# Transposes of an attention step ahead of its score blocks, another ring for one row tile, and two operand addresses moved

## The chip, the cores and the metric

The kernel runs on one core of one Trainium2 chip, in one launch. The metric is the device time of one execution in microseconds (us). The kernel before takes 2876.37 us, the median of three runs (2876.22 to 2876.55).

## What is computed

One layer of a transformer for two streams, 256 context tokens and 2048 latent tokens, with parameters shared. Cut to what matters here:

```python
h = rms_norm(x, norm1_g) * (1 + sc1) + sh1
q, k, v, f = project(h, w_in, q_g, k_g)        # 4 heads x 2 halves x 64 | same | 4 x 128 | 4 x 128
# attention of a head: two score halves, one difference of softmaxes
s = einsum('bqhmd,bkhmd->bhmqk', q, k) * scale  # m = 0, 1; latent: 2048 queries, 2560 keys
p = softmax(s)
a = p[:, :, 0] - lam * p[:, :, 1]
o = einsum('bhqk,bkhe->bqhe', a, v)
# the other half of the width
spec = fft2(f, axes=(positions, 128 channels), norm='ortho').real
mix = concat([rms_norm(o) * (1 - lam_init), spec @ w_four]) @ w_out
x = x + g1 * mix
x = x + g2 * relu(h2 @ w1) ** 2 @ w2            # h2: the second norm of x
```

## The kernel before

All matrix work is fp32 or split in two fp32r parts (`h` for high, `l` for low), of which three products are added. The program runs in stages: modulation and projections of 18 token tiles of 128 rows (up to about 465 us), the Fourier half (465 to 526), attention of four heads (526 to some 1260), output projection, and an MLP in three parts (to 2873).

**Projection and Fourier.** `v_out` (L397) copies the value rows of a token tile out of PSUM (L402, ScalarE) into a row tile `vo` and stores it (L403, the SyncE queue, written SP or SPq). The row tile comes from the ring `t2`, six tiles of 2 KB a partition in the pool of the projection; another ring of the same pool, `ff`, has four tiles and holds the rows that the Fourier channels load and store (`fh`, `fo`, `mid`). The pool ends with the projection, and the tiles of the Fourier stage are laid over its addresses. The first subtraction of the Fourier stage, four instructions `d<-ss,ss` on VectorE (DVE) at L845 (`diff`), takes differences of loaded rows `ss`; TensorE (PE) then reverses rows (`rev<-d`, L859), transforms (`pabo`, L786; `py`, `pz`, L751 and L753), and ScalarE (ACT) and DVE combine (`yd`, L770, needs `yv`, L760). Between them lie the last transposed query and key rows of the projection: `pt<-ident,qo` (L900, PE) and `qkT_1l` (L660, DVE), of which `pz` takes over the PSUM bank.

**Attention.** A head works through eight groups of two query tiles. A group has four steps, one for each tile and score half, and a table of due times (from L1255 on: `add(time, function)`, sorted by time) writes out the order of every engine by hand. In a step:

- `fill` (L1071) computes five score blocks of 128 x 512, two matmuls each (L1080). A block takes one of five PSUM banks with the tag `S`, so a block waits for the `exp` of the same number of the step before to read its bank.
- `rowmax` (L1085, DVE) reduces each block, `comb` (L1088, DVE) joins the five, and `exp` (L1104, ACT) turns the five blocks into probabilities, which land in `P0s` for the first half and `P1s` for the second. They run during the next step.
- for the group before, `tr` (L1126) transposes blocks of the combined probabilities, four transposes at a time (L1135), into one of two PSUM banks `pts`; `ah` (L1142, ACT) and `al` (L1147, DVE) split them, and `mul` multiplies them with the values `Vs` (L93 to L95, called the V block here), two of the blocks in plain fp32 (`vf4s`, `vf14s`).
- in the first step of a group, `o1` copies the transposed output of an earlier group (`oTs`, L1172, ACT) and `o2` transposes it back (L1176, two transposes on PE).

By the table, PE does in every step: V block of the step before, block 0, first transposes, (in the first step `o2`), blocks 1 and 2, second transposes, blocks 3 and 4, (in every other step third transposes), V block.

I call the steps of a group first, second, third and fourth by the blocks that are filled in them: (tile 0, half 0), (tile 0, half 1), (tile 1, half 0), (tile 1, half 1).

**MLP.** In its first part (L1738, `mms`) every product of a 512-row slice p of the MLP's input takes 12 matmuls of 128 x 384 (L1749 to L1751), with the slice's tiles `mhh` and `mhl` as one operand. Seven slices and 48 output blocks give 336 products. The slices 1 and 6 have their tiles in the pool `hpa`.

`shift` (L83) allocates a tile that nothing uses, and so moves the addresses of all that is allocated after it in a pool.

Of the kernel before, what the change touches and what calls it, by code (L numbers as in the profile page):

```python
# [11 lines left out]
F32 = mybir.dt.float32  # L12
# [7 lines left out]
P = 128  # L20
# [21 lines left out]
def body(tc, a, out):  # L42
    nc = tc.nc
    ctx = ExitStack()
    with ctx:
# [210 lines left out]
        with ExitStack() as c1:  # L256
# [2 lines left out]
            pp = c1.enter_context(tc.tile_pool(name="p1p", bufs=2, space=PSUM))  # L259
            pps = c1.enter_context(tc.tile_pool(name="p0p", bufs=1, space=PSUM))  # L260
            N1 = NT // P

            def t2(nm):
                return p1.tile([P, 512], F32, tag="t2", name=nm, bufs=6)
# [132 lines left out]
            def v_out(i):  # L397
                s = 1 if i < 2 else 0
                n = i if s else i - 2
                ps = PJ.pop((i, 2))  # L400
                o = t2(f"vo{i}")
                nc.scalar.copy(o, ps)  # L402
                nc.sync.dma_start(out[3][n * P:n * P + P] if s else vs[n * P:n * P + P], o)  # L403
                return o
# [57 lines left out]
            with tc.manual_schedule():  # L462
# [134 lines left out]
                qk_post(0)  # L597
                v_split(1, 0, vo0, "v0")
                load(3)
            wm, LAST = None, N1 - 1  # L600
            sums = po.tile([P, 4, 2, 16], F32, tag="sums", name="sums", bufs=1)
            for i in range(1, LAST):
                mg = 3 + (i + 1) // 2
# [383 lines left out]
        with ExitStack() as c3_:  # L987
# [18 lines left out]
            class Head:  # L1006
# [15 lines left out]

                def load_v(self):
                    s, h, ak = self.s, self.h, self.ak
                    if not s and h == 1:
                        shift(ak, 224, "v")
                    self.V = ak.tile([P, self.nkt, 2, P], F32R, tag=f"V_{s}", name=f"V{self.nm}")
                    nc.sync.dma_start(f32(self.V), vd[s][h])
                    self.vf = {}
                    if not s:  # L1030
                        for kb in FULL:
                            t = ak.tile([P, 2, P], F32, tag=f"vf{kb}", name=f"vf{kb}{self.nm}")
                            r = (kb - 4) * P
                            nc.sync.dma_start(t, vs[r:r + 2 * P, self.hc].rearrange("(t p) e -> p t e", p=P))
                            self.vf[kb] = t
                        if h < 2:
                            shift(ak, (192, 32)[h], "k")

            class Group:
                def __init__(self, hd, g):  # L1040
# [244 lines left out]
            for h in range(H):  # L1285
# [17 lines left out]
                for g in range(hd.ng):  # L1303
                    gr = Group(hd, g)
                    add(base - (4 if h or g > 1 else 3) * T + 0.6 * u if base else -3.03 * T, gr.qload)
                    for st in range(4):
                        j, m = divmod(st, 2)
                        t0 = base + st * T
                        for b in range(hd.nbk):
                            add(t0 - T + (0.76 + 0.66 * b) * u, gr.fill, j, m, b)  # L1310
                            add(t0 - T + (1.26 + 0.66 * b) * u, gr.rowmax, j, m, b)
                            add(t0 + 0.66 * b * u, gr.exp, j, m, b)
                        add(t0 - 0.45 * u, gr.comb, j, m)
                        if m:
                            add(t0 + (4.5 if gr.last and j else 5.9) * u, gr.combine, j)
                            if gr.last and j:
                                add(t0 + T + 5.3 * u, gr.combine_v, j)
                    kbs = list(range(0, hd.nkt, 2))
                    for q in range(4):
                        w = base + (AVS + q) * T  # L1320
                        if q % 2 == 0:
                            order = [kbs.pop(0) for _ in range(2)]
                            tr_t, ah_t, al_t = [0.9, 2.2], [3.3, 3.8], [4.6, 5.2]
                        else:
                            order = [kbs.pop(0) for _ in range(3)]
                            tr_t, ah_t, al_t = [0.9, 2.2, 3.86], [3.3, 3.8, 4.4], [None, 4.6, 5.2]
                        for n, kb in enumerate(order):
                            add(w + tr_t[n] * u, gr.tr, kb)
                            add(w + (2.0 if gr.drain and kb == FULL[0] else ah_t[n]) * u, gr.ah, kb)
                            if al_t[n]:  # L1330
                                add(w + al_t[n] * u, gr.al, kb)
                            add(w + T + (3.9 + 0.01 * n) * u, gr.mul, kb)
                            if q == 3 and not n:
                                add(w + 3.95 * u, gr.mul_part, kb)
                    w = base + (AVS + 5) * T + 1.0 * u
                    for t, fn in ((0, gr.o1), (0.4, gr.o2), (0.75 if gr.last else 4.25, gr.o3), (8.5, gr.o4), (9.2, gr.o5), (9.6, gr.o6)):
                        if gr.last and t:
                            LASTO.append(fn)
                        else:
                            add(w + t * u, fn)  # L1340
                    base += 4 * T
# [124 lines left out]
        def h_parts(b, p):  # L1466

            src = HR.pop((b, p))
            pool = hpa if p in (1, 6) else hp[p]
            if pool is hpa and not b and p == 6:  # L1470
                shift(hpa, 32, "a")
            hi = pool.tile([P, 4, 384], F32R, tag=f"mhh{p}", name=f"mhh{b}_{p}")
            lo = pool.tile([P, 4, 384], F32R, tag=f"mhl{p}", name=f"mhl{b}_{p}")
            HO[b, p] = hi, lo
# [47 lines left out]
        LAST = seq[-1]  # L1522
# [611 lines left out]
```

## Time and profile before

| | |
|---|---|
| median of three runs | 2876.37 us |
| the profiled execution | 2874.63 us, span of its instructions 2872.8 us |
| TensorE matmuls busy | 2836.6 us, 99% of the span |
| VectorE, ScalarE, GpSimd busy | 70%, 54%, 37% of the span |
| granted TensorE clock, mean | 0.998 of full speed |
| Fourier stage | about 465 to 526 us |
| attention | about 526 to 1260 us; four steps in some 22.05 us |
| MLP, first part | 1477 to 2182 us |

A row of a timeline has the start in us from the span's start, the duration in us, the engine (PE matmul, PEld weight load, DVE, ACT, POOL, SP or SPq for the queue of SyncE), the line, the operation, output and inputs by the program's names, and the count of instructions that are drawn together. In brackets stands how long the engine was idle before, and what ended the wait. Matmuls overlap, so that the start of the next one tells more than a duration.

### The profile page before, as it was taken

Reading aid. Unit: us, or ns where it says so; the run is one execution under the profiler, and the core shown is the slowest. Engines: PE = TensorE matmul, PEld = TensorE weight load, DVE = VectorE, ACT = ScalarE, POOL = GpSimd, SP = SyncE. Lnnn points to the kernel's source line nnn. Section 1 sums busy time; section 2 is a strip of 40 time slices with the busy share of each in tenths; the row PEclk is TensorE's granted clock in tenths of the full one; section 3 lists DMA queues with packets and bytes.
Section 4 is the critical chain, followed back from the end, with each engine's and each line's share of the span. In section 5 each row is a group of like instructions: output and inputs, shape, how many; then the busy total and the mean of one; then the engine's idle time right before and its main releaser. Section 6 shows DMA issues by size and latency. Waiting matters only on the chain.

```text
span 2872.8 us, 43229 instructions
## 1 busy us (share of the span) xinstructions
PE 2836.6 (99%) x15109; PEld 2468.8 (86%) x15109; DVE 2018.6 (70%) x3393; ACT 1547.6 (54%) x3505; POOL 1071.2 (37%) x890
## 2 busy tenths in 40 slices
PE   8999999999999999999999999999999999999999
PEld 5888887688888888888889999999998888888887
DVE  7777776898988989864477777778775354345554
ACT  4333332798998989953355565556554332233221
POOL 1211113699998999942223333334332000000000
PEclk9999999999999999999999999999999999999999
DMA  7787877531211312036777676667657464445663
GB/s 284 218 208 207 228 201 212 188 113 38 72 69 45 114 38 97 22 112 209 233 222 232 222 248 225 214 229 235 227 179 248 141 203 142 139 143 180 206 207 110
DMA packets 392780, 492.94 MB, mean 172 GB/s; under 512 B 26467, under 2 KB 306384, under 8 KB 389490
## 3 DMA queue, kind: packets, MB, share of 16 engines
q1 hardware_dynamic: 387136, 479.73, 52.3%
q0 software_dynamic: 1872, 7.28, 0.8%
q10 hardware_dynamic: 3554, 3.17, 0.4%
q8 instruction: 119, 1.95, 0.3%
q14 instruction: 99, 0.81, 0.1%
HBM read 312.58 MB, written 179.59 MB: 171 GB/s over the span
## 4 chain that ended last, share of the span: by engine, by line
PE 54%; DVE 1%; DMA 0%; ACT 0%; issue 0%; POOL 0%; SPq 0%; DVEq 0%; POOLq 0%
PE ps L93 8%; PE ps L95 8%; PE ps L94 8%; PE pA L1751 2%; PE pA L1750 2%; PE pA L1749 2%; PE pB L1749 2%; PE pB L1750 2%; PE pB L1751 2%; PE pC L1750 2%; PE pC L1751 2%; PE pC L1749 2%; PE po L95 2%; PE po L93 2%; PE po L94 2%; PE pD L1751 1%
## 5 line engine op out<-in xcount | busy, mean ns | idle before, releaser
L1085 DVE TENSOR_REDUCE mxs<-Ss 128x1 f32<-128x512 f32 x636 | 413.6, 685 | 65.2 <-PE Ss L1080 53.8
L1420 DVE TENSOR_TENSOR sl<-sr,sh 128x768 fp32r<-128x768 f32 x168 | 161.8, 964 | 331.5 <-ACT sh L1419 331.1
L1120 POOL TENSOR_TENSOR P0s<-P0s,P1s 128x1024 f32<-128x1024 f32 (+2 forms) x128 | 378.3, 2955 | 10.7
L1419 ACT CAST sh<-sr 128x768 fp32r<-128x768 f32 x168 | 140.6, 838 | 418.3 <-PE ps L94 418.3
L1791 POOL TENSOR_TENSOR gs<-g,g 128x384 f32<-128x384 f32 x48 | 69.7, 1452 | 470.2 <-ACT g L1761 410.2
L1104 ACT ACTIVATE P1s<-Ss,mxs 128x512 f32<-128x512 f32 x318 | 215.4, 694 | 36.3 <-DVE mxs L1088 36.3
L93 PE MATMUL pj<-wh,hh 128*128 128x512 f32 x576 | 228.0, 396 | 2.9 <-DVE hh L553 2.0
L93 PE MATMUL ps<-thT,sh 128*128 128x512 f32 x585 | 227.6, 389 | 0.0
L94 PE MATMUL ps<-tlT,sh 128*128 128x512 f32 x585 | 227.6, 389 | 0.0
L95 PE MATMUL ps<-thT,sl 128*128 128x512 f32 x585 | 227.6, 389 | 0.0
L94 PE MATMUL pj<-wl,hh 128*128 128x512 f32 x576 | 227.1, 394 | 0.5 <-DVE wl L514 0.5
L95 PE MATMUL pj<-wh,hl 128*128 128x512 f32 x576 | 225.8, 392 | 0.0
L1104 ACT ACTIVATE P0s<-Ss,mxs 128x512 f32<-128x512 f32 x318 | 214.4, 691 | 5.4 <-DVE mxs L1088 4.8
L1080 PE MATMUL Ss<-KS1s,Qs 128*128 128x512 f32 x636 | 196.5, 421 | 5.5 <-ACT P0s L1104 3.5
L1080 PE MATMUL Ss<-KS0s,Qs 128*128 128x512 f32 x636 | 197.1, 423 | 2.4 <-ACT P1s L1104 2.4
L1135 PEld LDWEIGHTS pts<-ident,P0s 128*128 128x128 f32 x1280 | 158.3, 140 | 43.1 <-ACT ahs L1142 2.7
L1135 PE MATMUL pts<-ident,P0s 128*128 128x128 f32 x1280 | 191.0, 273 | 0.7 <-ACT P1s L1104 0.7
L1760 ACT ACTIVATE g<-uz 128x384 f32<-128x384 f32 x144 | 75.9, 527 | 201.9 <-DVE uz L1783 175.7
L1119 POOL TENSOR_SCALAR P1s<-P1s,tots 128x1024 f32<-128x1024 f32 (+2 forms) x128 | 171.8, 1342 | 5.8
L1147 DVE TENSOR_TENSOR als<-pts,ahs 128x512 fp32r<-128x512 f32 x256 | 165.9, 681 | 7.0 <-ACT ahs L1142 6.7
L93 PE MATMUL ps<-ophT,sh 128*128 128x512 f32 x423 | 164.7, 389 | 1.1 <-DVE uz L1783 1.1
L1142 ACT CAST ahs<-pts 128x512 fp32r<-128x512 f32 x256 | 147.1, 611 | 32.7 <-PE pts L1135 32.7
(536 smaller groups left out, 8089.9 us busy)
## 6 DMA issues: line engine op xcount, KB each, us to landing
sr<-sd SPq DMA_DIRECT2D x84, 768.0 KB
a<-in_w SPq DMA_DIRECT2D x184, 256.0 KB
sd<-gs SPq DMA_DIRECT2D x192, 192.0 KB
sd<-g SPq DMA_DIRECT2D x144, 192.0 KB
wm<-in_w_mod SPq DMA_DIRECT2D x32, 512.0 KB
Qs<-qd SPq DMA_DIRECT2D x32, 512.0 KB
b<-in_w SPq DMA_DIRECT2D x64, 256.0 KB
b<-tsum SPq DMA_DIRECT2D x64, 256.0 KB
```

Source lines behind the costliest of these rows:

```text
L93: nc.tensor.matmul(ps, lh, rh, start=first, stop=False)
L94: nc.tensor.matmul(ps, lh, rl, start=False, stop=False)
L95: nc.tensor.matmul(ps, ll, rh, start=False, stop=last)
L1080: nc.tensor.matmul(S[:, :w], self.Q[:, x, m, j * P:j * P + P], self.hd.KS[m][:, b * 512:b * 512 + w], start=(x == 0), stop=(x == 1))
L1085: nc.vector.tensor_reduce(self.mx[j][:, m, b:b + 1], self.S[j, m, b], axis=AX.X, op=ALU.max)
L1104: nc.scalar.activation(dst, S, AF.Exp, bias=self.mx[j][:, m, 6:7], accum_out=self.sm[j][:, m, b:b + 1])
L1119: nc.gpsimd.tensor_scalar(p, p, tot[:, 3:4], 0.0, op0=ALU.mult, op1=ALU.add)
L1120: nc.gpsimd.tensor_add(d, d, p)
L1135: nc.tensor.transpose(pt[:, c:c + P], self.p0[j][:, (kb + t) * P:(kb + t + 1) * P], ident)
L1749: nc.tensor.matmul(ps, wh[:, c], hh[:, k, :], start=first and k == 0, stop=False, skip_group_check=True)
L1750: nc.tensor.matmul(ps, wh[:, c], hl[:, k, :], start=False, stop=False, skip_group_check=True)
L1751: nc.tensor.matmul(ps, wl[:, c], hh[:, k, :], start=False, stop=k == 3, skip_group_check=True)
```

## The change

Same instructions, same counts. What differs:

1. **Order of PE in attention.** The due time of the first transposes of a step goes from 0.9 to 0.7 (in fifths of a step), and so in front of that of block 0 (0.76). In 121 of the 128 steps of the four heads the first four transposes stand ahead of block 0 now. The order of the other engines is the same.
2. **The row tile of the last token tile.** The value rows `vo` of token tile 17 come from the ring `ff` and not from `t2`. Its address goes from 22496, where the Fourier stage puts the output of its first subtraction, to 64672, which the stage writes first at about 498 us (`ys`).
3. **Addresses.** Three unused tiles go away. With them the values `Vs` of the second and the fourth head (heads 1 and 3) go from 160960 to 160992, their `vf4s` and `vf14s` 32 bytes up as well, their `KS0s` and `KS1s` 256 bytes up, and the tiles of slice 1 of the MLP from 120576 and 126720 to 120608 and 126752. Modulo 64, `Vs`, `vf` and slice 1 go from 0 to 32, where all other large operands of TensorE's matmuls lie in both kernels; `KS` stays at 32.

```diff
+            LAST = N1 - 1
...
-                o = t2(f"vo{i}")
+                o = p1.tile([P, 512], F32, tag="ff", name=f"vo{i}", bufs=4) if i == LAST else t2(f"vo{i}")
                 nc.scalar.copy(o, ps)
                 nc.sync.dma_start(out[3][n * P:n * P + P] if s else vs[n * P:n * P + P], o)
...
-            wm, LAST = None, N1 - 1
+            wm = None
...
                 def load_v(self):
                     s, h, ak = self.s, self.h, self.ak
-                    if not s and h == 1:
-                        shift(ak, 224, "v")
...
-                        if h < 2:
-                            shift(ak, (192, 32)[h], "k")
+                        if h == 0:
+                            shift(ak, 192, "k")
...
-                            tr_t, ah_t, al_t = [0.9, 2.2], [3.3, 3.8], [4.6, 5.2]
+                            tr_t, ah_t, al_t = [0.7, 2.2], [3.3, 3.8], [4.6, 5.2]
...
-                            tr_t, ah_t, al_t = [0.9, 2.2, 3.86], [3.3, 3.8, 4.4], [None, 4.6, 5.2]
+                            tr_t, ah_t, al_t = [0.7, 2.2, 3.86], [3.3, 3.8, 4.4], [None, 4.6, 5.2]
...
             pool = hpa if p in (1, 6) else hp[p]
-            if pool is hpa and not b and p == 6:
-                shift(hpa, 32, "a")
```

In the changed file the lines of attention stand one line earlier (L1080 becomes L1079, L1135 becomes L1134), those of the Fourier stage one later (L845 becomes L846), those of the MLP three earlier.

PE before, at the start of a second step (group 4 of head 2, tile 0, half 1). The end of the V block is followed by block 0 (`x2`: two matmuls), then the first transposes `pts`.

```order
L95 MATMUL po<-ahs_2_2_10920,Vs_8771 128x256
L1080 MATMUL Ss_4_0_1_0_11027<-KS1s_8469,Qs_4_10719 128x512 x2
L1135 MATMUL pts_2_10_11030<-ident,P0s_2_0_10418 128x128
L1135 MATMUL pts_2_10_11030<-ident,P0s_2_1_10569 128x128
L1135 MATMUL pts_2_10_11030<-ident,P0s_2_0_10418 128x128
L1135 MATMUL pts_2_10_11030<-ident,P0s_2_1_10569 128x128
L1080 MATMUL Ss_4_0_1_1_11045<-KS1s_8469,Qs_4_10719 128x512 x2
L1080 MATMUL Ss_4_0_1_2_11050<-KS1s_8469,Qs_4_10719 128x512 x2
```

PE after the change, at the same place.

```order
L95 MATMUL po<-ahs_2_2_10918,Vs_8769 128x256
L1134 MATMUL pts_2_10_11025<-ident,P0s_2_0_10416 128x128
L1134 MATMUL pts_2_10_11025<-ident,P0s_2_1_10567 128x128
L1134 MATMUL pts_2_10_11025<-ident,P0s_2_0_10416 128x128
L1134 MATMUL pts_2_10_11025<-ident,P0s_2_1_10567 128x128
L1079 MATMUL Ss_4_0_1_0_11030<-KS1s_8467,Qs_4_10717 128x512 x2
L1079 MATMUL Ss_4_0_1_1_11043<-KS1s_8467,Qs_4_10717 128x512 x2
L1079 MATMUL Ss_4_0_1_2_11048<-KS1s_8467,Qs_4_10717 128x512 x2
```

Blocks 0, 1 and 2 stand in a row now, with all four transposes ahead of them. The third and the fourth step change in the same way.

PE before, at the start of a first step (the same group), where `o2` (L1176) stands between the first transposes and block 1.

```order
L95 MATMUL po<-ahs_1_18_10859,Vs_8771 128x256
L1080 MATMUL Ss_4_0_0_0_10948<-KS0s_8467,Qs_4_10719 128x512 x2
L1135 MATMUL pts_2_4_10951<-ident,P0s_2_0_10418 128x128
L1135 MATMUL pts_2_4_10951<-ident,P0s_2_1_10569 128x128
L1135 MATMUL pts_2_4_10951<-ident,P0s_2_0_10418 128x128
L1135 MATMUL pts_2_4_10951<-ident,P0s_2_1_10569 128x128
L1176 MATMUL po<-ident,oTs_1_10956 128x128 x2
L1080 MATMUL Ss_4_0_0_1_10963<-KS0s_8467,Qs_4_10719 128x512 x2
```

PE after the change, at the same place.

```order
L95 MATMUL po<-ahs_1_18_10857,Vs_8769 128x256
L1134 MATMUL pts_2_4_10943<-ident,P0s_2_0_10416 128x128
L1134 MATMUL pts_2_4_10943<-ident,P0s_2_1_10567 128x128
L1134 MATMUL pts_2_4_10943<-ident,P0s_2_0_10416 128x128
L1134 MATMUL pts_2_4_10943<-ident,P0s_2_1_10567 128x128
L1079 MATMUL Ss_4_0_0_0_10951<-KS0s_8465,Qs_4_10717 128x512 x2
L1175 MATMUL po<-ident,oTs_1_10954 128x128 x2
L1079 MATMUL Ss_4_0_0_1_10961<-KS0s_8465,Qs_4_10717 128x512 x2
```

The transposes went ahead of block 0; `o2` stays between block 0 and block 1.

DVE before, at the start of the Fourier stage, with the waits of each row (queues of DMA and engines; no order of the rows changes here).

```order
L660 TENSOR_TENSOR qkT_0l<-pt_0_4704,qkT_0h 128x512 [waits Activation_49]
L845 TENSOR_TENSOR d_3_4713<-ss_4583,ss_4589 128x512 [waits DMAHW3_49,DMAHW4_49,DMAHW0_49,DVE_49]
L845 TENSOR_TENSOR d_2_4712<-ss_4583,ss_4589 128x512 [waits DMAHW7_49]
L845 TENSOR_TENSOR d_0_4710<-ss_4580,ss_4586 128x512 [waits DMAHW5_49,DMAHW1_49]
L845 TENSOR_TENSOR d_1_4711<-ss_4580,ss_4586 128x512 [waits DMAHW6_49,DMAHW2_49]
```

DVE after the change, at the same place.

```order
L660 TENSOR_TENSOR qkT_0l<-pt_0_4704,qkT_0h 128x512 [waits Activation_49]
L846 TENSOR_TENSOR d_3_4713<-ss_4583,ss_4589 128x512 [waits DMAHW4_49,DMAHW0_49]
L846 TENSOR_TENSOR d_2_4712<-ss_4583,ss_4589 128x512 [waits DMAHW7_49,DMAHW3_49]
L846 TENSOR_TENSOR d_0_4710<-ss_4580,ss_4586 128x512 [waits DMAHW5_49,DMAHW1_49]
L846 TENSOR_TENSOR d_1_4711<-ss_4580,ss_4586 128x512 [waits DMAHW6_49,DMAHW2_49,DVE_49]
```

The first row no longer waits for the store of `vo` (its wait on the queue `DMAHW3`); the waits of the four for the loads of `ss` are left. In exchange ACT's copy into `vo` (L402) waits for one queue more, that of the last access to its new place in the ring `ff`.

## The prediction

> **What bounds the kernel now.** I read the page first, then the busy time by stages, then the waits and timelines of the three places that the change touches. The page's first line has TensorE at 99%.
>
> ```profile
> PE 2836.6 (99%) x15109; PEld 2468.8 (86%) x15109; DVE 2018.6 (70%) x3393; ACT 1547.6 (54%) x3505; POOL 1071.2 (37%) x890
> ```
>
> Two windows (length, then busy us and count of PE, PEld, DVE, ACT, POOL, then the granted clock, the DMA share and GB/s): one of the few microseconds at the start of the Fourier stage, one of the MLP's first part.
>
> ```profile
> 487.00:490.00 3.00, 3.00 (x7) 2.03 (x6) 2.97 (x5) 0.00 (x0) 0.00 (x0) 0.50 0.00 0
> 1700.00:2300.00 600.00, 598.92 (x3289) 578.39 (x3288) 411.01 (x613) 331.35 (x601) 175.76 (x136) 1.00 0.64 213
> ```
>
> The MLP is TensorE's alone: what a matmul there gets shorter, the end gets earlier. In the 3 us after 487 TensorE is busy too, but at a granted clock of 0.50. So a busy TensorE can still be sped up by a better pace, and the rest of its time is in short waits.
>
> **The row tile of the last token tile.** The timeline at the start of the Fourier stage:
>
> ```profile
> 477.76 0.69 DVE L660 TENSOR_TENSOR qkT_0l<-pt,qkT_0h 128x512 fp32r<-128x512 f32 x1 [0.64 <-ACT qkT_0h L659]
> 479.85 1.89 PE L786 MATMUL pabo<-s,rv 128*128 128x256 f32 x8
> 482.11 0.56 SPq L403 DMA_DIRECT2D vs<-vo  x1
> 483.29 0.60 PE L900 MATMUL pt<-ident,qo 128*128 128x128 f32 x4
> 483.49 0.59 ACT L760 COPY yv<-pz 128x512 f32<-128x512 f32 x1 [0.27 <-PE pz L753]
> 485.67 2.50 DVE L845 TENSOR_TENSOR d<-ss,ss 128x512 f32<-128x512 f32 x4 [7.21 <-DMA vd<-v17h]
> 486.50 1.60 PE L859 MATMUL rev<-d,jm 128*128 128x512 f32 x2 [2.61 <-DVE d L845]
> 487.90 3.12 PE L786 MATMUL pabo<-s,rv 128*128 128x256 f32 x8
> 489.29 0.69 DVE L770 TENSOR_TENSOR yd<-yu,yv 128x512 f32<-128x512 f32 x1
> 492.35 0.68 DVE L660 TENSOR_TENSOR qkT_1l<-pt,qkT_1h 128x512 fp32r<-128x512 f32 x1
> 493.09 1.12 PE L753 MATMUL pz<-abo,cw 128*128 128x512 f32 x2 [1.21 <-DVE qkT_1l L660]
> ```
>
> DVE ends L660 at 478.45 and stands still until 485.67, because its next output lies on `vo`, whose store is issued only at 482.11 (the row names a neighbouring store, of `v17h`, issued at the same place). TensorE pays twice, 2.61 us before `rev` and 1.21 before `pz`. It pays a third time in pace: the same eight matmuls `pabo` took 1.89 us at 479.85 and 3.12 at 487.90, in the window with the clock at 0.50. That is 2.61 + 1.21 + 1.23 = **5.05 us**. The same worked through DVE: the four subtractions start at 478.45. What lies between them and `yd` (489.29 - 485.67 = 3.62) would end at 482.07, but `yd` needs `yv`, which is there at 484.08. From `yd` to the start of `qkT_1l` it is 3.06 and 0.68 more, which makes 487.82. TensorE is free after `pt` at 483.89 and needs from `rev` to `pz` what it needed from 486.50 to 491.88, 5.38, less 1.23: 488.04 where it was 493.09. So DVE comes just in time, and 5.05 stands. Behind this place all starts that much earlier, since SyncE's loads for attention queue behind stores that wait for `qkT_1l`. If the slow pace stays, it is 3.82; if only the first wait goes, 2.61. The new wait of ACT's copy into `vo` costs nothing as far as I see: the ring's rows were stored long before. Bounds 2.6 and 5.6 (`rev` too runs in the slow stretch).
>
> By the Trainium skill, "TensorE: Matmul & The Clock Gate", Part 1, the clock drops to half only after an idle window of some 3.4 us. The gap here is 2.61 us, and the rows show half the clock right behind it. By that rule alone the gap would not be the reason, and the sum for this place would be 3.82.
>
> **The transposes ahead of block 0.** A first step of attention, then a second and a third:
>
> ```profile
> 938.38 0.73 PE L1080 MATMUL Ss<-KS0s,Qs 128*128 128x512 f32 x2
> 938.90 0.37 ACT L1172 COPY oTs<-po 128x256 f32<-128x256 f32 x1
> 939.39 0.38 PE L1176 MATMUL po<-ident,oTs 128*128 128x128 f32 x2
> 940.00 0.30 PEld L1080 LDWEIGHTS Ss<-KS0s,Qs 128*128 128x128 f32 x2 [0.20 <-ACT P1s L1104]
> ...
> 943.19 0.69 ACT L1104 ACTIVATE P0s<-Ss,mxs 128x512 f32<-128x512 f32 x1
> 943.66 0.28 PE L95 MATMUL po<-ahs,Vs 128*128 128x256 f32 x1
> 944.02 0.73 PE L1080 MATMUL Ss<-KS1s,Qs 128*128 128x512 f32 x2
> 944.53 0.68 ACT L1104 ACTIVATE P0s<-Ss,mxs 128x512 f32<-128x512 f32 x1
> 944.94 1.18 PE L1080 MATMUL Ss<-KS1s,Qs 128*128 128x512 f32 x4
> 945.96 0.60 PE L1135 MATMUL pts<-ident,P0s 128*128 128x128 f32 x4
> ...
> 949.56 0.64 PE L1080 MATMUL Ss<-KS0s,Qs 128*128 128x512 f32 x2
> 950.04 0.60 PE L1135 MATMUL pts<-ident,P0s 128*128 128x128 f32 x4
> 950.24 0.69 DVE L1085 TENSOR_REDUCE mxs<-Ss 128x1 f32<-128x512 f32 x1 [0.19 <-PE Ss L1080]
> 950.39 1.18 PE L1080 MATMUL Ss<-KS0s,Qs 128*128 128x512 f32 x4
> 951.15 1.29 DVE L1085 TENSOR_REDUCE mxs<-Ss 128x1 f32<-128x512 f32 x2 [0.22 <-PE Ss L1080]
> 951.76 0.94 PE L1080 MATMUL Ss<-KS0s,Qs 128*128 128x512 f32 x3
> ```
>
> In the second step the V block's last matmul starts at 943.66, and block 0 only at 944.02: it waits for the first `exp`, which ends at 943.88, 0.14 earlier. The transposes could run in that hole. But the wait is not gone, it moves: the third `exp` (944.53) ends at 945.21, so block 2 can't start before 945.35. Before, block 2 followed block 1 (944.94) after some 0.46 to 0.51 (two blocks take 1.02 until 945.96), at 945.40 to 945.45. At most 0.05 to 0.1 us is gained, and a pair of matmuls that waited takes longer than one that didn't (0.73 in the row of 944.02, 0.64 in that of 949.56), which costs 0.09. Net **0**.
>
> In the first step `o2` sits behind block 0 and waits for `oTs`, which ACT ends at 939.27; `o2` started at 939.39. And block 2 waits there for its `exp` already, 0.20 at 940.00. Net **0** again. In the third and fourth step block 0 doesn't wait; it moves 0.35 later (950.39 - 950.04, the length of the four transposes), block 1 stays. Its row maximum moves from 950.24 to 950.59, three more at a pitch of 0.60 (1.29 for two, 0.69 for one) bring the fourth to 952.39, and that one can't start before 951.76 + 0.76 = 952.52 anyway (0.76: from 950.39 to 951.15). The delay is caught up with 0.13 to spare: **0**. I take 0 for the reorder, with 3 us to both sides for the unknown pace at the new seams, and the rivals beyond that.
>
> **The addresses.** `o2` marks the same point of each group: with 939.39 above, three groups of head 2 and four of head 3; under them the same matmul with `Vs` in a stretch of head 1 (720 to 840) and of head 2 (900 to 1000), by shape, and the starts of three neighbouring products of the MLP, of slices 1, 6 and 3:
>
> ```profile
> 1005.50 0.38 PE L1176 MATMUL po<-ident,oTs 128*128 128x128 f32 x2
> 1095.78 0.38 PE L1176 MATMUL po<-ident,oTs 128*128 128x128 f32 x2
> 1184.16 0.38 PE L1176 MATMUL po<-ident,oTs 128*128 128x128 f32 x2
> ...
> L94 PE MATMUL po<-als,Vs 128*128 128x256 f32 x86 | 24.2, 281 | 0.0
> L94 PE MATMUL po<-als,Vs 128*128 128x256 f32 x72 | 20.0, 278 | 0.0
> ...
> 1814.35 0.34 PE L1749 MATMUL pA<-mhh,ophW 128*128 128x384 f32 x1
> 1816.47 0.34 PE L1749 MATMUL pB<-mhh,ophW 128*128 128x384 f32 x1
> 1818.55 0.34 PE L1749 MATMUL pC<-mhh,ophW 128*128 128x384 f32 x1
> ```
>
> A group takes (1005.50 - 939.39) / 3 = 22.04 us in head 2, with `Vs` at 32 modulo 64, and (1184.16 - 1095.78) / 4 = 22.10 in head 3, with 0. For the 16 groups of heads 1 and 3 that is 16 x 0.058 = **0.9 us**, if the address is the reason. The matmul itself is 3 ns longer; twelve a step in 64 steps make 2.3, the upper bound; the lower one is 0. The product of slice 1 takes 2.12 us, its neighbour of slice 6 takes 2.08. With 48 products of slice 1 and no wait around them that is **1.9 us**, between 0 and 2.4.
>
> **The sum.** 5.05 + 0 + 0.93 + 1.92 = 7.9 us. The profiled execution took 2874.63 (span 2872.8); 2866.7 would be its like. It stands 1.74 under the median of the runs shown, 2876.37, so the median goes to **2868.5**.
>
> **Rivals.** *The hole is filled* (0.13): the `exp`s don't hold up blocks 1 and 2 after all, and the waits of block 0 vanish. The table of waits from 560 to 1257 has
>
> ```profile
> PEld Ss L1080 <- ACT P0s L1104: 12.0, 37, 0.7
> PEld Ss L1080 <- ACT P1s L1104: 7.3, 40, 0.2
> ```
>
> or 19.3 us in 77 waits, 0.25 each; in the 32 second steps, where nothing else gates, that is 8 us: 2860.5. Against it speaks the pitch of the `exp`s, 0.67 us (943.19 to 944.53 for two), against 0.46 for a block. *The row maxima come late* (0.10): between them DVE has subtractions of `al` and the scaling of sums, and its spare in the third and fourth step is 0.13 us. If their pitch is over 1.93 / 3 = 0.64, the four can't catch up. At worst the whole 0.35 goes into `comb` and the next step's `exp`s, two steps a group, 32 groups: 22 us more, 2891; at a pitch of 0.69 it is 0.14 a step, 9 us, 2877.5. Half way, 2884. That is **slower than before**. *The addresses do nothing* (0.12): slice 1 and heads 1 and 3 are slower for another reason, and 2.85 us are missing: 2871.4. Beside it stands the Trainium skill, "SBUF — State Buffer", Specifications: it counts cost by lines of 16 bytes, and 0 and 32 modulo 64 both begin one. By that rule the edit is worth nothing; the 3 ns and 0.04 us above speak against it. *The Fourier stage gives less* (0.12): the slow pace stays, or DVE finds a next late load; 2.6 to 3.8 there, so 2869.7 to 2870.9.
>
> **How the numbers follow.** The forecast has 0.53. A difference under 0.2%, 5.75 us, is about what can't be told from no change; 2870.6 is that border. Of the forecast's share 0.44 lies below it, 0.09 above; the filled hole adds 0.13 to faster; the addresses split 0.04 faster and 0.08 same, the Fourier case 0.05 and 0.07; the late maxima give 0.08 slower, 0.02 same. Faster 0.66, same 0.26, slower 0.08. The range goes from 2859 (the filled hole, with bounds) to 2878 (the late maxima at their mild end) and leaves out their worse half and a gain beyond the hole.
>
> **What would show it.** DVE's L846 starts near 478.5 with no wait for a DMA, and no stretch of clock 0.50 follows; `pz` starts near 488. In attention the wait of the weight load for block 0 is gone and a like one stands before block 1 or 2, with `o2` still 0.1 behind `oTs`; a group still takes 22.05 us in head 2, and 22.05 in head 3. Slice 1 takes 2.08 us. I am wrong on the reorder if a group gets shorter by over 0.1 us, or if `comb` of the fourth step comes later behind its last block.

## The result, and the profile after

The changed kernel takes **2864.01 us**, the median of five runs (2863.21 to 2865.55); the kernel before took 2876.37 in five runs beside it (2874.70 to 2876.55). The ratio is 0.9958, with a 95% interval of 0.9944 to 0.9973: faster by 12.4 us. A second set of runs gave 2867.39 against 2876.01 (0.9968, 0.9955 to 0.9981), 8.6 us. Forecast were 7.9. The profiled execution took 2863.21 with a span of 2861.4, 11.4 less than the span before.

The page of the kernel after. TensorE is as full as before.

```profile
PE 2832.7 (99%) x15109; PEld 2456.2 (86%) x15109; DVE 2017.4 (71%) x3393; ACT 1547.7 (54%) x3505; POOL 1071.1 (37%) x890
```

Where the 11.4 us went, from the starts of the same TensorE instructions in the two profiled executions:

| stage | after, less before (us) |
|---|---|
| start to 465 (projections) | -1.58 |
| Fourier stage | -6.35 |
| first step of attention to the first `o2` | -1.6 |
| the rest of attention | 0.0 |
| MLP, first part | -1.83 |
| the rest | 0.0 |

The start of the Fourier stage, in the timeline of the kernel after (start, duration, engine, line, operation):

```profile
476.78 2.49 DVE L846 TENSOR_TENSOR d<-ss,ss 128x512 f32<-128x512 f32 x4
...
478.46 0.59 ACT L761 COPY yv<-pz 128x512 f32<-128x512 f32 x1 [0.15 <-PE pz L754]
...
480.39 0.69 DVE L771 TENSOR_TENSOR yd<-yu,yv 128x512 f32<-128x512 f32 x1
...
480.56 0.56 SPq L404 DMA_DIRECT2D vs<-vo  x1
...
481.71 0.60 PE L901 MATMUL pt<-ident,qo 128*128 128x128 f32 x4
...
481.91 0.59 ACT L761 COPY yv<-pz 128x512 f32<-128x512 f32 x1 [0.27 <-PE pz L754]
...
482.14 1.02 PE L860 MATMUL rev<-d,jm 128*128 128x512 f32 x2
...
483.00 1.89 PE L787 MATMUL pabo<-s,rv 128*128 128x256 f32 x8
...
483.47 0.68 DVE L661 TENSOR_TENSOR qkT_1l<-pt,qkT_1h 128x512 fp32r<-128x512 f32 x1
...
485.59 1.02 PE L754 MATMUL pz<-abo,cw 128*128 128x512 f32 x2
```

The four subtractions start with no wait, 3.8 us ahead of the store of `vo` that held them up before. `rev` follows `pt` at once, and `pabo` has its 1.89 us. The same place by windows (busy us of PE, PEld, DVE, ACT, POOL, then the granted clock), full clock throughout:

```profile
480.00:483.00 3.00, 3.00 (x11) 1.52 (x10) 2.93 (x5) 2.25 (x4) 1.84 (x2) 1.00 0.95 211
483.00:486.00 3.00, 3.00 (x12) 2.09 (x11) 2.75 (x5) 0.80 (x2) 3.00 (x7) 1.00 1.05 290
```

Attention: a second step after the change, with the blocks 0, 1 and 2 (two matmuls each) and the wait of block 2 (PEld is the weight load that holds the matmul back).

```profile
934.29 0.63 PE L1134 MATMUL pts<-ident,P0s 128*128 128x128 f32 x4
...
934.67 1.82 PE L1079 MATMUL Ss<-KS1s,Qs 128*128 128x512 f32 x6
...
935.75 0.30 PEld L1079 LDWEIGHTS Ss<-KS1s,Qs 128*128 128x128 f32 x2 [0.33 <-ACT P0s L1103]
```

Block 0 no longer waits, and block 2 waits 0.33 us for its `exp`. The table of waits in attention (550 to 1247; us in total, times, longest) has the same releasers with more in them:

```profile
PEld Ss L1079 <- ACT P0s L1103: 17.3, 54, 0.4
PEld po L1175 <- ACT oTs L1171: 12.7, 31, 0.6
PEld Ss L1079 <- ACT P1s L1103: 9.4, 49, 0.4
...
PE pts L1134 <- DVE alp L1234: 1.3, 4, 0.3
```

Blocks wait 26.7 us in 103 waits, where it was 19.3 in 77, and `o2` waits 31 times for `oTs`, 12.7 us. Yet the groups are not longer: the starts of `o2`, three groups apart in head 2 and four in head 3,

```profile
929.72 0.44 PE L1175 MATMUL po<-ident,oTs 128*128 128x128 f32 x2
995.73 0.44 PE L1175 MATMUL po<-ident,oTs 128*128 128x128 f32 x2
1018.70 0.44 PE L1175 MATMUL po<-ident,oTs 128*128 128x128 f32 x2
1086.15 0.44 PE L1175 MATMUL po<-ident,oTs 128*128 128x128 f32 x2
1174.31 0.44 PE L1175 MATMUL po<-ident,oTs 128*128 128x128 f32 x2
```

make (995.73 - 929.72) / 3 = 22.00 us a group and (1174.31 - 1086.15) / 4 = 22.04, against 22.04 and 22.10. The weight loads wait longer and at more places, and yet the groups don't get longer, which reads as a pace set elsewhere, by the `exp`s; o1_late, below, tries that. One group of each head is an exception: 1018.70 - 995.73 = 22.97, where the same group took 1028.07 - 1005.50 = 22.57. The end of that group in the kernel before:

```profile
1028.07 0.38 PE L1176 MATMUL po<-ident,oTs 128*128 128x128 f32 x2
```

The timeline of its slow step after the change, in head 0:

```profile
655.06 0.69 DVE L1084 TENSOR_REDUCE mxs<-Ss 128x1 f32<-128x512 f32 x1 [0.95 <-PE Ss L1079]
655.67 0.68 DVE L1234 TENSOR_TENSOR alp<-ptp,ahp 128x512 fp32r<-128x512 f32 x1
...
656.50 0.63 PE L1134 MATMUL pts<-ident,P0s 128*128 128x128 f32 x4 [0.32 <-DVE alp L1234]
```

and the same step before:

```profile
664.32 0.69 DVE L1085 TENSOR_REDUCE mxs<-Ss 128x1 f32<-128x512 f32 x1 [0.48 <-PE Ss L1080]
664.93 0.68 DVE L1235 TENSOR_TENSOR alp<-ptp,ahp 128x512 fp32r<-128x512 f32 x1
665.52 2.66 DVE L1085 TENSOR_REDUCE mxs<-Ss 128x1 f32<-128x512 f32 x4
665.76 0.63 PE L1135 MATMUL pts<-ident,P0s 128*128 128x128 f32 x4
```

Here, in the fourth step ahead of group 5, two banks of transposes come first (`ptp`, then `pts`). Block 0 is later, DVE's first row maximum with it (it waits 0.95 instead of 0.48), then `alp`, which must read `ptp` before the second transposes may overwrite it; they wait 0.32 us where they did not.

The MLP: three neighbouring products of the slices 1, 6 and 3.

```profile
1803.94 0.34 PE L1746 MATMUL pA<-mhh,ophW 128*128 128x384 f32 x1
...
1806.02 0.34 PE L1746 MATMUL pB<-mhh,ophW 128*128 128x384 f32 x1
...
1808.10 0.34 PE L1746 MATMUL pC<-mhh,ophW 128*128 128x384 f32 x1
```

Slice 1 takes 2.08 us, as its neighbour, where it took 2.12.

### The profile page after: what moved, and what is told of

Read it like the earlier page. It is cut to its first block, busy times and chain, and to the rows that moved or that the text cites. A ratio compares the mean times of both kernels' runs of the same rounds, so it can differ in the third digit from the quotient of the medians.

```text
span 2861.4 us, 43230 instructions
## 1 busy us (share of the span) xinstructions
PE 2832.7 (99%) x15109; PEld 2456.2 (86%) x15109; DVE 2017.4 (71%) x3393; ACT 1547.7 (54%) x3505; POOL 1071.1 (37%) x890
## 4 chain that ended last, share of the span: by engine, by line
PE 54%; DVE 1%; DMA 0%; ACT 0%; issue 0%; SPq 0%; POOL 0%; DVEq 0%; POOLq 0%
PE ps L93 8%; PE ps L94 8%; PE ps L95 8%; PE pB L1748 2%; PE pB L1746 2%; PE pB L1747 2%; PE pC L1748 2%; PE pA L1748 2%; PE pC L1746 2%; PE pA L1747 2%; PE pA L1746 2%; PE pC L1747 2%; PE po L93 2%; PE po L95 2%; PE po L94 2%; PE pD L1748 1%
## 5 line engine op out<-in xcount | busy, mean ns | idle before, releaser
L1084 DVE TENSOR_REDUCE mxs<-Ss 128x1 f32<-128x512 f32 x636 | 405.6, 685 | 66.3 <-PE Ss L1079 56.1
L1134 PE MATMUL pts<-ident,P0s 128*128 128x128 f32 x1280 | 191.6, 273 | 4.5 <-DVE als L1146 1.9
L1079 PE MATMUL Ss<-KS1s,Qs 128*128 128x512 f32 x636 | 189.1, 421 | 1.4 <-ACT P0s L1103 1.4
L1079 PE MATMUL Ss<-KS0s,Qs 128*128 128x512 f32 x636 | 190.1, 419 | 0.4 <-ACT P1s L1103 0.4
L1134 PEld LDWEIGHTS pts<-ident,P0s 128*128 128x128 f32 x1280 | 151.4, 140 | 35.8 <-issue 4.2
L95 PE MATMUL ps<-ophT,sl 128*128 128x512 f32 x423 | 164.6, 389 | 0.0
```

Of the source, the lines that this page charges most:

```text
L95: nc.tensor.matmul(ps, ll, rh, start=False, stop=last)
L1079: nc.tensor.matmul(S[:, :w], self.Q[:, x, m, j * P:j * P + P], self.hd.KS[m][:, b * 512:b * 512 + w], start=(x == 0), stop=(x == 1))
L1084: nc.vector.tensor_reduce(self.mx[j][:, m, b:b + 1], self.S[j, m, b], axis=AX.X, op=ALU.max)
L1134: nc.tensor.transpose(pt[:, c:c + P], self.p0[j][:, (kb + t) * P:(kb + t + 1) * P], ident)
```

## The experiments

My theory after the result: the ring gives the 6.3 us of the Fourier stage (wait, half clock, second wait); the reorder moves waits and gives nothing; the addresses give the MLP's 1.8 us; the rest is chance. Rivals: the reorder gives the 1.6 us at the start of attention; the half clock has nothing to do with the gap; the place of the operands modulo 64 is not what counts. Each ratio is to runs of the kernel before on the same chip, which differ from set to set: 2874.24 (22 runs, 2871.75 to 2877.66) for the first four, 2876.01 (9 runs) for the next four, 2875.24 (7 runs) for the last three.

| kernel | us | ratio to before, 95% | runs |
|---|---|---|---|
| swap_only | 2873.98 | 0.9999 (0.9989 to 1.0008) | 10 |
| ring_only | 2868.60 | 0.9978 (0.9968 to 0.9987) | 10 |
| no_swap | 2867.27 | 0.9972 (0.9961 to 0.9983) | 7 |
| fill_gap | 2874.58 | one run | 1 |
| after_again | 2867.39 | 0.9968 (0.9955 to 0.9981) | 5 |
| swap_but | 2865.84 | 0.9964 (0.9950 to 0.9978) | 5 |
| o1_late | 2862.71 | 0.9952 (0.9937 to 0.9967) | 4 |
| addr_flip | 2868.72 | one run | 1 |
| both | 2861.89 | 0.9955 (0.9939 to 0.9972) | 4 |
| o1_old_order | 2863.80 | 0.9960 (0.9945 to 0.9975) | 4 |
| addr_64 | 2868.29 | one run | 1 |

**The order alone** (swap_only: the kernel before with the new due time).

```diff
-                            tr_t, ah_t, al_t = [0.9, 2.2], [3.3, 3.8], [4.6, 5.2]
+                            tr_t, ah_t, al_t = [0.7, 2.2], [3.3, 3.8], [4.6, 5.2]
...
-                            tr_t, ah_t, al_t = [0.9, 2.2, 3.86], [3.3, 3.8, 4.4], [None, 4.6, 5.2]
+                            tr_t, ah_t, al_t = [0.7, 2.2, 3.86], [3.3, 3.8, 4.4], [None, 4.6, 5.2]
```

> Only the first transposes of a step go ahead of block 0; ring and addresses as before. Theory (the exps, one every 0.67 us, hold up block 1 or 2 as they held up block 0): within 2 us of the kernel before in all; a usual group of attention stays within 0.1 us of its 22.05 to 22.10 us, one step in each head gets some 0.45 us longer, and what is won comes from the first steps of attention (0 to 1.5 us, if the half clock at 558 to 562 goes). Rival (the holes in front of block 0 get filled): 4 to 8 us faster, spread over all groups, 0.15 to 0.25 us each.

No difference: 0.9999. From the first `o2` to the output projection it is 0.77 us longer than before, with the same slow group in each head (22.96 to 23.02). The waits are those of the kernel after:

```profile
PEld Ss L1080 <- ACT P0s L1104: 17.3, 54, 0.4
PEld po L1176 <- ACT oTs L1172: 12.6, 32, 0.6
```

At the start of attention this run too is 1.6 us shorter than the profiled one of before; the next two kernels show what that is.

**The ring alone** (ring_only: the kernel before with the one row tile moved).

```diff
-                o = t2(f"vo{i}")
+                o = p1.tile([P, 512], F32, tag="ff", name=f"vo{i}", bufs=4) if i == N1 - 1 else t2(f"vo{i}")
```

> Only the row tile of the last token tile comes from the other ring. Theory: the Fourier stage gets 6.3 us shorter (2.6 of TensorE's wait before rev, 1.2 to 1.4 before pz, the rest because the half clock behind the wait is gone), and all other stages keep their length, but for the half clock at 558, which may go or stay, as its place on the clock's grid moves: 6 to 8 us faster. Rival (the gain of the whole change came from the reorder): 3 to 4 us faster at most, with the half clock still there behind 486.

Behind `pt`, the Fourier stage gets 6.25 us shorter up to the next pair of `rev` (6.35 to its end). The medians differ by 5.6, a little under the 6 to 8 that I expected, and the two profiled executions by 3.8. The projections took 1.6 us longer in this execution, and ahead of `pt` DVE waited 2.7 us more for loads (`E`, L718, for `rv<-frev`), which delayed TensorE by 2.6. That load was as late in no_swap (3.0 us of TensorE), less so in o1_old_order (1.3), and hardly or not at all in the seven other profiled executions with the new ring. The three late ones are just those that have the new ring with the old order. No trace shows how an order that begins with attention, at 526 us, could reach back to 465. It may be chance, but that isn't shown. The start of attention is 1.47 shorter here as well, without the new order, so the new order is not needed for that.

**Everything but the order** (no_swap: the kernel after with 0.9 in place of 0.7 in both lists).

> The changed kernel with the old order of the transposes: ring and addresses alone. Theory: 8 to 10 us faster than before (6.3 Fourier, 1.8 slice 1 of the MLP, 0 to 0.9 in heads 1 and 3), so within 2 us of the changed kernel; if the address of V counts, a group of heads 1 and 3 takes 22.05 us here where it took 22.10, else 22.10. Rival (the reorder carries the gain): 4 to 6 us behind the changed kernel.

2867.27, 7.0 us under the kernel before, where I expected 8 to 10: the late loads cost 3.0 us in the profiled execution, and the start of attention gains nothing. The MLP gains 1.84, the Fourier stage 6.25; usual groups of heads 1 and 3 take 22.04 us in the mean, where they take 22.10 in ring_only; from the first `o2` to the output projection it is 0.95 shorter than before, where the kernel after is 0.04 shorter. So the new order costs 0.9 us in this stretch, as between swap_only and ring_only (0.77 + 0.12). The start of attention is as long as before, though all but the order is that of after. Its windows show why (columns as above):

```profile
555.20:558.60 3.40, 3.40 (x12) 2.78 (x11) 1.70 (x4) 2.36 (x6) 3.40 (x2) 0.53 0.02 5
```

There is a stretch of half clock, as in the kernel before at this place:

```profile
555.20:558.65 3.45, 1.44 (x9) 1.14 (x9) 2.94 (x6) 2.43 (x8) 3.19 (x5) 1.00 0.45 154
558.65:562.05 3.40, 3.40 (x11) 2.73 (x11) 1.92 (x4) 2.27 (x6) 3.40 (x2) 0.50 0.02 5
```

and none in the kernel after:

```profile
546.90:550.30 3.40, 1.54 (x9) 0.99 (x8) 2.68 (x6) 2.38 (x7) 3.22 (x4) 1.00 0.47 157
550.30:553.70 3.40, 3.40 (x22) 2.65 (x21) 3.21 (x6) 3.07 (x9) 3.32 (x3) 1.00 0.02 5
```

The gap ahead of it is 1.99 to 2.01 us with the old order and 1.83 to 1.86 with the new one. Of the five traces with the old order three have the half clock here, of the eight with the new one none. So the new order may save a part of this 1.6 us, which would make up for the 0.9 that it costs behind; the runs don't settle that.

**The gap filled with idle work** (fill_gap: the kernel before, where the four transposes of the last key rows are made seven times, so that TensorE has no gap ahead of `rev`; nothing else changes).

```diff
-                for h in range(H):
+                for h in range(H * (7 if m else 1)):
+                    h %= H
```

> The kernel before, with the four transposes pt of the last key rows done seven times over (the same result each time), so that TensorE works through the wait for rev. Theory (half clock follows an idle TensorE): no clock of 0.50 behind 486, the eight pabo take 1.89 us and not 3.12, while pz still starts at 493.1, held by VectorE, so the time stays within 0.5 us of before, the half clock at 558 apart. Rival (something else at this place slows TensorE): 0.50 again, and 3.12 us for the eight.

The timeline and a window of this kernel:

```profile
484.32 3.22 PE L901 MATMUL pt<-ident,qo 128*128 128x128 f32 x28
485.91 2.50 DVE L845 TENSOR_TENSOR d<-ss,ss 128x512 f32<-128x512 f32 x4 [6.42 <-DMA vs<-vo]
487.38 1.02 PE L859 MATMUL rev<-d,jm 128*128 128x512 f32 x2
488.24 1.89 PE L786 MATMUL pabo<-s,rv 128*128 128x256 f32 x8
...
492.60 0.68 DVE L660 TENSOR_TENSOR qkT_1l<-pt,qkT_1h 128x512 fp32r<-128x512 f32 x1
...
493.33 1.12 PE L753 MATMUL pz<-abo,cw 128*128 128x512 f32 x2 [2.34 <-DVE qkT_1l L660]
```

```profile
486.90:490.30 3.40, 3.40 (x17) 2.57 (x16) 3.37 (x7) 0.66 (x2) 0.00 (x1) 1.00 0.21 39
```

DVE is as late as before, but `rev` and `pabo` run at full clock. This is one execution, but it does not stand alone: the two traces with a gap ahead of `rev` (before, 2.61 us, and swap_only, 2.47) have the half clock behind it, and the eleven without the gap, by the ring or by the filling, do not. So the gap was the cause of the half clock. The time gained goes into the wait of `pz`, 2.34 instead of 1.21, since DVE comes no earlier; behind that gap the clock stays at full. And the releaser is named here as the store of `vo` itself.

**The changed kernel again** (after_again: no edit).

> The changed kernel once more, beside the kernel before on the same chip. Theory (fixed parts: 6.25 us in the Fourier stage, 1.84 in slice 1, 0.2 to 0.5 by the address of V, minus 0.6 to 0.9 that the reorder costs in the heads; the rest is chance in the loads of the projection and in the half clock): 7 to 9 us faster than before in the median. Rival (the first five runs' 12 us belong to the change): 11 to 13 us faster again.

8.6 us in the medians, 8.64 between its profiled execution and that of before. By stages against that one: projections +1.56, Fourier stage -6.9, start of attention -1.6, rest of attention +0.2, MLP -1.83. The two profiled executions of this one kernel lie 3.1 us apart in the projections alone, which is most of the distance between 12.4 and 8.6.

**The old order in the one slow step** (swap_but).

```diff
-                            tr_t, ah_t, al_t = [0.7, 2.2], [3.3, 3.8], [4.6, 5.2]
+                            tr_t, ah_t, al_t = [0.9 if g == 5 and not q else 0.7, 2.2], [3.3, 3.8], [4.6, 5.2]
```

> The changed kernel with the old order in the one step of each head in which the context tokens' transposes stand in front as well. Theory (there the row maximum of block 0 comes 0.4 us later, the subtraction alp queues behind it, and the second transposes wait for its bank): that step gets 0.4 us shorter in each head, 1.6 to 1.8 us in all against the changed kernel. Rival (that step is slow for another reason, its third transposes or its score blocks): no change in its length, 0 us.

The group takes 22.5 us instead of 22.97, and from the first `o2` to the output projection it is 1.6 us less than in the kernel after, 0.4 a head.

**`oTs` and `o2` later** (o1_late: in the kernel after, behind the `exp`s of the first blocks).

```diff
-                    for t, fn in ((0, gr.o1), (0.4, gr.o2), (0.75 if gr.last else 4.25, gr.o3), (8.5, gr.o4), (9.2, gr.o5), (9.6, gr.o6)):
+                    for t, fn in ((0 if gr.last else 1.7, gr.o1), (0.4 if gr.last else 2.6, gr.o2), (0.75 if gr.last else 4.25, gr.o3), (8.5, gr.o4), (9.2, gr.o5), (9.6, gr.o6)):
```

> The changed kernel with the copy oTs on ScalarE behind the five exps of a first step in place of between the second and the third, and o2 behind block 4. Theory (the pace of the exps, not TensorE's order, sets a first step): exps 2 to 4 come 0.25 us earlier, the wait before o2 is gone, and a usual group takes 21.75 to 21.9 us in place of 22.0: 4 to 7 us faster than the changed kernel. Rival (TensorE's own work and order set the step): within 0.05 us of 22.0 a group, within 1.5 us in all.

The starts of `o2` are now (head 2, three groups; head 3, four):

```profile
931.00 0.38 PE L1175 MATMUL po<-ident,oTs 128*128 128x128 f32 x2
996.71 0.38 PE L1175 MATMUL po<-ident,oTs 128*128 128x128 f32 x2
...
1086.68 0.38 PE L1175 MATMUL po<-ident,oTs 128*128 128x128 f32 x2
1174.41 0.38 PE L1175 MATMUL po<-ident,oTs 128*128 128x128 f32 x2
```

21.90 and 21.93 us a group, 0.10 and 0.11 less, and the median is 4.7 us under that of after_again, on the same chip. ACT's copy `oTs` (0.37 us) stood between the `exp`s for which the blocks wait: two `exp`s started 0.91 us apart across it and 0.66 without it. Taken out of there, it shortens the group, though TensorE's work is the same. That is what the theory of the `exp`s' pace asks for, at the small end of what I expected. The edit also moves `o2` on TensorE, behind block 4, and ends its wait for the copy; no run moves one without the other, so the share of the `exp`s alone is argued and not shown. Some of it was lost again: a new stretch of half clock stands at 1221 to 1225, where attention ends.

**Both** (both: swap_but and o1_late together).

> The changed kernel with both edits: the old order in the one step of each head (as in swap_but) and oTs behind the five exps (as in o1_late). Theory (the two act on different steps): their gains add, 1.8 and 3 to 4 us, so 4.5 to 6 us faster than the changed kernel, 11 to 14 us faster than before. Rival (both free the same slack): not over 4 us faster than the changed kernel.

2861.89, the lowest time of all, 13 us under the kernel before. Usual groups take 21.81 to 21.95 us, and the slow group of each head 22.35 to 22.44, where it is 22.88 to 22.90 in o1_late: in the trace the two gains add. By the intervals of the whole time it is not told apart from o1_late.

**`oTs` later, and the old order** (o1_old_order: no_swap with the edit of o1_late).

> Block 0 ahead of the first transposes as in the kernel before (ring and addresses as changed), and oTs behind the five exps. Theory (the exps set the pace, the order of block 0 and the transposes is worth nothing either way): a usual group takes 21.9 us as in o1_late, and without the slow step of each head the kernel ends 1 to 2 us ahead of o1_late, 4 to 6 us ahead of the changed one. Rival (the new order is what lets the earlier exps be used): 22.0 us a group, within 1.5 us of the changed kernel.

Groups of 21.88 to 22.0, typically 21.95, where o1_late has 21.92 and both 21.89 in the mean. So with `oTs` out of the way the new order is worth 0.03 to 0.06 us a group, less than 2 us in all; with `oTs` in its old place it is 0.03 (22.05 in no_swap, 22.03 in the kernel after). Against the kernel before the median gains 11.4 us, o1_late 13.3, so it does not end ahead of o1_late as I expected; the intervals don't tell the two apart.

**The place modulo 64 turned round** (addr_flip: the kernel after, with the tiles of slice 6 at 0 modulo 64, 132864 and 139008, those of slice 1 at 32 modulo 64 as in the kernel after, but at 120544 and 126688, and `KS` of heads 1 and 3 at 0 modulo 64).

```diff
+                    if not s and h == 1:
+                        shift(ak, 32, "v")
...
+            if pool is hpa and not b and p == 6:
+                shift(hpa, 32, "a")
...
+            if pool is hpa and not b and p == 6:
+                shift(hpa, 32, "c")
```

> The changed kernel with the tiles of slice 6 of the MLP at 0 modulo 64 (slice 1 stays at 32), and KS0s, KS1s of heads 1 and 3 at 0 modulo 64. Theory (a large operand at 0 modulo 64 costs TensorE time): products of slice 6 take 2.12 us and those of slice 1 2.08, the MLP's first part gets 1.8 us longer than in the changed kernel; for KS the matmuls of score blocks get longer in heads 1 and 3 by up to 3 ns each. Rival (slice 1 was slower for its place in the order): slice 6 stays at 2.08, 0 us.

The opposite of the rule: slice 6, moved to 0, keeps its pace, and slice 1, still at 32, gets slow. Its products of the slices 1, 6 and 3 are

```profile
1808.78 0.34 PE L1752 MATMUL pA<-mhh,ophW 128*128 128x384 f32 x1
...
1810.89 0.34 PE L1752 MATMUL pB<-mhh,ophW 128*128 128x384 f32 x1
...
1812.97 0.34 PE L1752 MATMUL pC<-mhh,ophW 128*128 128x384 f32 x1
```

2.11 us for slice 1 and 2.08 for slice 6. The MLP is 0.59 shorter than before, not 1.83. `KS` at 0 is no slower either (in heads 1 and 3 some 232 ns from matmul to matmul, 233 in the kernel after, waits left out). "0 modulo 64" is not what counts.

**64 lower** (addr_64: the kernel after, with slice 1 alone at 120544, still 32 modulo 64, and `Vs`, `vf`, `KS` of heads 1 and 3 64 lower, `Vs` at 160928, still 32 modulo 64).

```diff
-                        if h == 0:
-                            shift(ak, 192, "k")
+                        if h < 2:
+                            shift(ak, (192, 64)[h], "k")
...
+            if pool is hpa and not b and p == 6:
+                shift(hpa, 64, "a")
```

> The changed kernel with slice 1's tiles 64 bytes lower (120544, as in addr_flip, still 32 modulo 64) while slice 6 stays, and Vs, vf and KS of heads 1 and 3 64 bytes lower. If what counts is the address modulo 64: slice 1 stays at 2.08 us a product, V's matmuls in heads 1 and 3 at 115.5 to 116 ns, as in the changed kernel. If slice 1's own place counts in another way: 2.11 us as in addr_flip, 1.2 us in all. If slice 6's place made slice 1 slow in addr_flip: 2.08.

Slice 1 is slow though slice 6 stands where it was:

```profile
1808.52 0.34 PE L1748 MATMUL pA<-mhh,ophW 128*128 128x384 f32 x1
...
1810.62 0.33 PE L1748 MATMUL pB<-mhh,ophW 128*128 128x384 f32 x1
```

2.10 us. The MLP is 0.53 shorter than before. In the V blocks of heads 1 and 3 a matmul with `Vs` starts 118.9 and 119.0 ns after the one before (mean of the distances under 140 ns), against 118.1 and 118.2 before and 116.1 and 115.7 after; heads 1 and 3 are 0.4 us each longer than after. So the place of an operand does set the pace, and a step of 64 changes it, which "modulo 64" excludes. What I have is a list: `Vs` fast at 160992, slow at 160960 and 160928; slice 1 fast at 120608, slow at 120576 and 120544; slice 6 fast at 132896 and 132864. Which property of the address counts stays open.

## Why the prediction was right, and where it was not

**The Fourier stage: right in its mechanism, 5.05 forecast, 6.25 measured.** All three terms are there in every kernel with the new ring. The gap ahead of `rev` gives 2.78 (2.61 forecast), the wait of `pz` 1.38 (1.21), both a little more than the idle time alone. The pace was mis-sized: I took 1.23, the loss of `pabo` alone, and put `rev` into the upper bound. Measured from start to start, the pair of `rev` gains 0.54 and the eight `pabo` 1.22, 1.76 in all, about half of the 3.40 us at half clock, which is what such a stretch must cost. A last 0.33 comes from `pz` to the next pair of `rev`, and 0.10 more inside that pair, which makes the 6.35 of the table. One step was false and happened not to matter: "`yd` needs `yv`, which is there at 484.08". That `yv` (481.91 in the trace after) is the next one. `yd` ran at 480.39, ahead of it, and `qkT_1l` was done at 484.15, 1.44 us before `pz`. DVE is not just in time; TensorE's own work bounds this place.

**The clock.** I let the half clock count as a result of the gap, against the rule of the Trainium skill ("TensorE: Matmul & The Clock Gate", Part 1) that an idle window of some 3.4 us is needed. fill_gap and the kernels with the new ring show the gap to be the cause. Taken as a gap of that length, the rule does not hold here; 2.61 us idle inside a window were enough, and 2.01 ahead of 558.65. In the same part, the Trainium skill has the windows run freely at 3413 ns; the stretches of before begin 71.7 us apart (487.0 and 558.6), 21 times 3.41, which agrees. What counts is how much of a gap lies inside one window. I summed up the time without a matmul window by window on that grid, from 450 to 2850 us in all thirteen traces: the seven windows with 1.90 us or more are followed by half clock, all others have 1.72 or less, and none of them is.

**The reorder: 0 forecast, 0.9999 measured alone.** The waits moved to block 2 and to `o2` as worked out, and none of the hole was won. Two small things lie under the zero. Usual groups are shorter by about 0.03 us. The one step of each head with two banks of transposes is 0.45 longer, 1.8 us in all; I worked the third and fourth step from a step without `alp`, and there the first row maximum of the late block 0 does hold up what is behind it. This is a form of the rival of the late row maxima, in 4 steps, not in 64. Net, between kernels that differ only in the order, it costs 0.9 us from the first `o2` on; ahead of that it may save a part of the half clock at 558.

**Slice 1: 1.92 forecast, 1.84 measured. `Vs`: 0.93 forecast, some 0.7 measured** (from the first `o2` to the output projection no_swap is 0.82 us shorter than ring_only, and the kernel after 0.82 shorter than swap_only; 0.52 and 0.67 of that lie in heads 1 and 3, but heads 0 and 2, where no address changes, differ by up to 0.21 each, so the size is rough). The sizes hold because they came from the pace of neighbours that were fast. My reason, that 0 modulo 64 is the slow place, is false by addr_flip and addr_64. Nor do lines of 16 bytes explain it (the Trainium skill, "SBUF — State Buffer", Specifications): all the places tried begin one, and they differ by some 3 ns a matmul in `Vs`. By my reason a place 64 lower than the changed one, at 32 modulo 64 as well, would give the same gain; in addr_64 it loses 1.3 us of it in the MLP.

**The sum.** The parts that come back wherever their edit is made add up to 6.25 + 1.84 + 0.7 - 0.9 = 7.9 us. That this is the forecast number is luck: an underrated Fourier stage covers an overrated `Vs` and the slow steps. The first set of runs shows 4 to 5 us more. In its profiled execution 1.6 of it stand ahead of 465, where no part of the change does any work (the second time it was 1.56 the other way), and 1.6 in the half clock at 558 that fell away. I named neither as an uncertainty. That second stretch was in front of me in the trace of before, and also that the gap ahead of it was near the length that counts.

**Not settled:** what in an address sets the pace; why the loads `rv<-frev` came late in ring_only, no_swap and o1_old_order; whether a given execution gets the stretch at 558. Of thirteen traces three have it (before, no_swap, fill_gap), all with the old order; ring_only and o1_old_order, with the old order and the same gap of 2.00 us, don't, since there a border of the grid cuts the gap (at most 1.64 us in one window of ring_only).

## What to carry to other kernels

A wait of TensorE costs its own length and then, if the clock falls, half of a whole window of 3.4 us behind it: look at the granted clock in the slices right after a gap, and price all that runs in them. Where many waits stand on one engine's pace (here the `exp`s), moving TensorE's work between them moved the waits and won next to nothing; taking a copy out of that engine's chain (with the work that waits for it) shortened the group. An effect that was read from neighbours may be forecast in size, but its rule needs a try at a third place before it is used to choose addresses.

## What I had not expected of the hardware

- The stretches of half clock inside the kernel are some 3.4 us long (twice that, 6.8, at 31 to 32 us in six of the thirteen traces) and have their own grid. In the kernel before they follow 1.99 us (ahead of 33), 2.01 and 2.61 us idle; in the kernel after none follows 1.86 us (at 549.13) or 1.61. But in o1_late and both one follows 1.90, and in fill_gap none follows 2.34. So whether a gap of 1.5 to 2.5 us costs another 1.6 depends on where it falls. They also come at 434 to 439 in four of the traces (fill_gap, swap_but, addr_flip, addr_64), where the passage from 431 to 445 takes 2.0 to 2.4 us more than in the trace of before; there windows with 1.35 to 1.75 us idle were followed by it, so the idle time alone is not the whole rule. It fits with this that runs of the kernel before spread from 2871.75 to 2877.66 in one set; that they cause the spread was not tried.
- The distance between matmuls depends on the place of the operand in a partition, already for moves of 32 and 64 bytes: 115.5 to 119.0 ns for `Vs`, which is loaded as weights (128x128), and 173.3 to 176.9 ns for slice 1, which is the other operand (128x384), in the means. In the slow place of the kernel before, the twelve distances of a product have a fixed pattern, 178, 175, 180, 174 ns three times over within 1 ns, product after product; at the fast place all are 173 or 174.
